# Sample rows through a DRAM scratch, a reordered key and value lane, denser squares in the first norm, and spreads by transposes, in a hybrid decoder step

## The chip, the core and the metric

The kernel runs on one core of a Trainium2 chip. The metric is the device time of one execution in microseconds (us). The engines run side by side and wait for one another only through semaphores: PE (TensorE, matmuls and transposes), DVE (VectorE), ACT (ScalarE), POOL (GpSimd), and SP (SyncE), which here issues every DMA.

## The reference

One layer of a decoder is computed for 256 prompt tokens and for 8 sample tokens (one new token for each of 8 sequences), together 264 columns. Cut to what matters here:

```python
# mixing sub-layer: x <- x + concat(out_A, out_B) @ w_out
proj = rmsnorm(x) @ w_in                         # [u | v_A | q | k | v | g]
out_A = gelu(u) * chunk_spatial_mix(layernorm(gelu(v_A)))
# retention, 8 heads of 128; for a sample token b and head h:
state[b] = gamma_h * state[b] + outer(k[b], v[b])     # 128 x 128
ret[b] = q[b] @ state[b]
out_B = silu(g) * groupnorm(ret)
# cross-attention, 4 heads of 512, 256 memory tokens; each sample token has its own cache
q = rmsnorm(x) @ w_cq
s[b] = cache_k[b] @ q[b] * 512 ** -0.5           # 256 scores
o[b] = softmax(s[b]) @ cache_v[b]
x = x + o @ w_co
# MLP and the last norm
x = x + relu(rmsnorm(x) @ w_ff1) ** 2 @ w_ff2
y = rmsnorm(x)
```

For the prompt, memory keys and values are computed from `mem_prompt` with `w_ck` and `w_cv`; they are outputs too, as are the retention states.

## The kernel before

**Weights.** Activations lie transposed: features on the 128 partitions, the 264 tokens along the free axis (sample tokens first, columns 0 to 7). All weight matrices are cut into chunks of 256 x 512 (512 KB); there are 512 of them in a fixed order: `w_in` (12 groups of 8 chunks, in the order v, q, k, q, k, v, vA, vA, g, g, u, u), `w_out`, `w_cq`, `w_ck` and `w_cv` in turn for four heads, `w_co`, then the MLP. `emit_dma` loads a chunk six ahead into one of five raw buffers, `emit_hi` casts it to fp32r on ACT, and `emit_lo` subtracts that on DVE to get the remainder; both are written two to three chunks ahead, into four buffers each. Every product is then three fp32r matmuls: high times high, high times low, low times high (L152 to L154 in `group_act`, L176 to L178 in `group_mem`). A group ends with four accumulators in PSUM, out of five banks; `evict` empties them on DVE and ACT, and the next group needs those banks.

**Order.** Between matmuls stand *points*, one after each six weight matmuls of `group_act`. At each point `run_point` (L210) advances every due generator of `chains`, then at most one of `tasks`, then issues due stores. A generator's `yield n` lets n points pass, a bare `yield` three. Tasks with a `lane` run in turn. All engines have their instructions in this written order, SP its DMAs too: an instruction that waits holds up what stands behind it on its engine.

**First norm.** The chunks of x are squared without the norm's factor, which is multiplied in behind the projection. `square_x` (L325) squares four tiles of 128 x 1056 on ACT and adds them on DVE; `column` sums over partitions with matmuls against ones and takes the power -1/2 on POOL; `tables` (L370) spreads the factor over the partitions (`spread`, L275: one matmul for each of three token blocks, the column broadcast as weights against the identity) and multiplies the rotary tables by it. Query and key evictions (`ev_rope`, L523) need those tables.

**Retention** (`retention`, L569) is one generator for each head, two lanes (`r0`, `r1`). For the sample tokens it transposes 8 columns of k and q into rows, casts them to a high part (rows 0 to 7 of `kq`) and a low part (rows 32 to 39), and then for each token a matmul with the selection column `sel[:, b]` broadcast (L619) puts row b, high plus low, on all 128 partitions of a PSUM tile `bc`. Two DVE instructions for each token then update the state (L622) and multiply it by q with a sum (L625).

**Sample attention** (`sample_attn`, L807) is one generator for each head in the lane `kv`. It makes split rows `qs` of the head's query in the same way; for each token a matmul (L820) spreads the row into `qb`, and two DVE products with the cached key tile (L823) give the scores. After a softmax the probabilities become split rows `pst`, spread by L843 into `pb`, and four DVE products with the cached value tile (L846) give the output. Key and value tiles (512 KB each) are loaded three ahead by `kv_fill` (L749), eight keys then eight values of each head in turn. Each key token takes five points, each value token four.

**Prompt attention** (`prompt_attn`) runs as a task put in front, once a head's memory keys and values are there. Before the seventh chunk of `w_co` all tasks are run out by `flush`.

Of the kernel before, what the change touches and what calls it, by code (L numbers as in the profile page):

```python
# [30 lines left out]
def build(tc, I, O):  # L31
# [5 lines left out]
    with cst as cst, wpool as wpool, spool as spool, tpool as tpool, psum as psum:  # L37
        with tc.manual_schedule():
            _emit(tc, cst, wpool, spool, tpool, psum, I, O)


def _emit(tc, cst, wpool, spool, tpool, psum, I, O):
# [41 lines left out]
    sel = cst.tile([128, 8], F32R, name="sel")  # L84
# [115 lines left out]
    def store(dst, src, delay=10):  # L200
        stores.append((now[0] + delay, dst, src))
# [8 lines left out]
    def run_point():  # L210
# [23 lines left out]
    class Stats:  # L234
# [40 lines left out]
        def spread(self, out, tok=TOK):  # L275
            ps = misc([128, self.n], "rsb")
            for i, (c0, n) in enumerate(tok):
                pe.matmul(ps[:, c0:c0 + n], lhsT=self.col[:, i:i + 1].broadcast_to([128, 128]),
                          rhs=ident[:, 0:n], start=True, stop=True)
            if out is None:  # L280
                return ps
            act.copy(out, ps[:])
# [42 lines left out]
    def square_x():  # L325
        a = slot([128, 4, T], "sqa")
        act.activation(a[:], hT[0][:], AF.Square)
        yield
        for s in range(1, 4):
            b = slot([128, 4, T], "sqb")  # L330
            act.activation(b[:], hT[s][:], AF.Square)
            yield 2
            dve.tensor_tensor(out=a[:], in0=a[:], in1=b[:], op=ALU.add)
            yield
        dve.tensor_tensor(out=a[:, 0:2, :], in0=a[:, 0:2, :], in1=a[:, 2:4, :], op=ALU.add)
        dve.tensor_tensor(out=st1.acc[:], in0=a[:, 0, :], in1=a[:, 1, :], op=ALU.add)
        yield 3
        st1.column()
        yield 4
        tables()  # L340
        for m in R4:
# [8 lines left out]
    def clear():  # L350
        zt = half("zt")
        dve.memset(zt[:], 0.0)
        S["kq"] = [S["rpool"].tile([128, 256], F32R, name="kq", tag="kq", bufs=2) for _ in range(2)]
        yield
        for i in range(2):
            act.copy(S["kq"][i][:], zt[:, 0:256])
        dve.tensor_tensor(out=sel[:], in0=ident[:, 0:8], in1=ident[:, 32:40], op=ALU.add)
# [127 lines left out]
    mix = {}  # L485
# [27 lines left out]
    def ev_rope(which, g):  # L513
        def ev(ps):
# [10 lines left out]
            def gen():  # L525
# [7 lines left out]
                if which == "k" and g == 0:  # L533
                    retentions(0)
# [33 lines left out]

    def retention(h):  # L569
# [6 lines left out]

        kn, vn = row("kn"), row("vn")
        sm = S["rpool"].tile([128, 384], F32, name="sm", tag="sm", bufs=2)
        kq = S["kq"][h % 2]
        tp = misc([128, 512], "tp")  # L580
# [3 lines left out]
        for i, src in enumerate((kt, qt)):  # L584
# [627 lines left out]
```

## Time and profile before

| what | value |
|---|---|
| time, median of 3 runs | 1603.66 us (1603.24 to 1604.05) |
| the profiled execution: time | 1604.01 us |
| its span, first to last instruction | 1602.1 us |
| mean granted clock of TensorE | 0.997 |
| busy: PE, DVE, ACT, POOL | 1587.7, 1040.8, 751.2, 124.1 us |
| moved by DMA | 326.15 MB, mean 204 GB/s |

How to read the views: the page's head gives the busy time of each engine with its share of the span and its instructions. The timeline lists instructions in the order of time: start, length, engine, line and operation, output and inputs, shape, count; in brackets the idle time of the engine before it and what ended it. The windows view gives, for stretches of time, each engine's busy time with its number of instructions, then the granted clock of TensorE, the mean busy share of the 16 DMA engines, and the rate. The list of groups has busy time and the mean length of one in ns, then the idle time just before such instructions and what ended it. The list of waits tells who waited for whom: total us, times, longest. The list of DMA issues gives count, size and the median us from issue to landing.

### The profile page before, as it was taken

To read this page: it belongs to the slowest core of one execution; us is meant where nothing else is said; L and a number is where in the kernel's file an instruction comes from. 1 tells how busy PE (TensorE), PEld (TensorE's weight loads), DVE (VectorE), ACT (ScalarE), POOL (GpSimd) and SP (SyncE) were. 2 spreads that over 40 slices of the span, in tenths; PEclk is the share of its full clock that TensorE was granted. 3 is DMA by queue.
4 is the path that set the end of the run, shared out by engine and by line. 5 is a ranking of instruction groups with operands and counts; after the bars stand their busy time and mean duration, and the time that the engine had idled before them with its cause. 6 is when DMAs were issued, how large, how long until landed. Compare 5 with 4: busy or idle time off the path is not lost.

```text
span 1602.1 us, 31005 instructions
## 1 busy us (share of the span) xinstructions
PE 1587.7 (99%) x12608; PEld 1560.0 (97%) x12608; DVE 1040.8 (65%) x1885; ACT 751.2 (47%) x1169; POOL 124.1 (8%) x111
## 2 busy tenths in 40 slices
PE   9999999999999999999999999999999999999997
PEld 8999999999999998999999999999999999999997
DVE  6677688678658777877655555555655555565555
ACT  6455566457444444444444543534444353444443
POOL 0242022010012201010000000000000000000000
PEclk9999999999999999999999999999999999999999
DMA  8566646465578887877555556565555655555552
GB/s 293 168 204 228 207 168 198 145 189 207 196 256 284 314 303 277 283 282 250 171 185 185 179 172 190 171 187 183 177 186 172 190 172 186 183 178 183 173 186 86
DMA packets 94222, 326.15 MB, mean 204 GB/s; under 512 B 10608, under 2 KB 15728, under 8 KB 94080
## 3 DMA queue, kind: packets, MB, share of 16 engines
q1 hardware_dynamic: 94080, 324.18, 60.8%
q8 instruction: 98, 1.61, 0.4%
q14 instruction: 44, 0.36, 0.1%
HBM read 313.03 MB, written 11.11 MB: 202 GB/s over the span
## 4 chain that ended last, share of the span: by engine, by line
PE 48%; issue 46%; DVE 1%; POOL 0%; ACT 0%; POOLq 0%; DVEq 0%
PE acc L152 13%; PE acc L153 13%; PE acc L154 13%; PE acc L178 2%; PE acc L177 2%; PE acc L176 2%; PE tp L96 1%; PE qb L820 0%; PE bc L619 0%; PE spp L474 0%; PE sc L898 0%; PE sc L896 0%; PE op L919 0%; PE sc L897 0%; PE op L921 0%
## 5 line engine op out<-in xcount | busy, mean ns | idle before, releaser
L1033 ACT CAST wh<-w 128x1024 fp32r<-128x1024 f32 (+1 forms) x513 | 536.1, 1045 | 712.1 <-PE acc L153 625.8
L1041 DVE TENSOR_TENSOR wl<-w,wh 128x1024 fp32r<-128x1024 f32 (+1 forms) x513 | 628.1, 1236 | 259.5 <-ACT wh L1033 257.5
L153 PE MATMUL acc<-h2l,wh 128*128 128x264 f32 x1024 | 291.2, 284 | 0.0
L152 PE MATMUL acc<-h2h,wh 128*128 128x264 f32 x1024 | 291.1, 284 | 0.0
L154 PE MATMUL acc<-h2h,wl 128*128 128x264 f32 x1024 | 290.6, 284 | 0.0
L153 PE MATMUL acc<-rl,wh 128*128 128x264 f32 x992 | 282.2, 284 | 0.0
L154 PE MATMUL acc<-rh,wl 128*128 128x264 f32 x992 | 282.1, 284 | 0.0
L152 PE MATMUL acc<-rh,wh 128*128 128x264 f32 x992 | 282.0, 284 | 0.0
L152 PE MATMUL acc<-xh,wh 128*128 128x264 f32 x768 | 225.1, 293 | 3.2 <-DVE ra L523 2.5
L154 PE MATMUL acc<-xh,wl 128*128 128x264 f32 x768 | 219.3, 286 | 0.4 <-DVE wl L1061 0.2
L153 PE MATMUL acc<-xl,wh 128*128 128x264 f32 x768 | 219.0, 285 | 0.1
L152 PEld LDWEIGHTS acc<-h2h,wh 128*128 128x128 f32 x1024 | 192.7, 188 | 0.0
L153 PEld LDWEIGHTS acc<-h2l,wh 128*128 128x128 f32 x1024 | 192.7, 188 | 0.0
L154 PEld LDWEIGHTS acc<-h2h,wl 128*128 128x128 f32 x1024 | 192.6, 188 | 0.0
L152 PEld LDWEIGHTS acc<-rh,wh 128*128 128x128 f32 x992 | 186.9, 188 | 0.0
L153 PEld LDWEIGHTS acc<-rl,wh 128*128 128x128 f32 x992 | 186.7, 188 | 0.0
L154 PEld LDWEIGHTS acc<-rh,wl 128*128 128x128 f32 x992 | 186.5, 188 | 0.0
L152 PEld LDWEIGHTS acc<-xh,wh 128*128 128x128 f32 x768 | 145.3, 189 | 5.8 <-DVE ra L523 3.2
L154 PEld LDWEIGHTS acc<-xh,wl 128*128 128x128 f32 x768 | 145.3, 189 | 0.9 <-DVE wl L1061 0.4
L153 PEld LDWEIGHTS acc<-xl,wh 128*128 128x128 f32 x768 | 145.5, 189 | 0.3 <-DVE xl L104 0.3
L951 DVE TENSOR_TENSOR hT<-hT,acc 128x264 f32<-128x264 f32 x124 | 53.2, 429 | 73.7 <-PE acc L154 73.7
L92 POOL TENSOR_TENSOR msr<-msv,neghalf 128x3 f32<-128x3 f32 (+1 forms) x5 | 7.7, 1547 | 991.5 <-DVE msv L265 739.1
(253 smaller groups left out, 2776.5 us busy)
## 6 DMA issues: line engine op xcount, KB each, us to landing
w<-in_w_ff_dram SPq DMA_DIRECT2D x256, 512.0 KB, 4.1
w<-in_w_in_dram SPq DMA_DIRECT2D x95, 512.0 KB, 3.8
w<-in_w_out_dram SPq DMA_DIRECT2D x32, 512.0 KB, 4.2
w<-in_w_cq_dram SPq DMA_DIRECT2D x32, 512.0 KB, 4.5
kv<-in_kN_dram SPq DMA_DIRECT2D x32, 512.0 KB, 5.2
kv<-in_vT_dram SPq DMA_DIRECT2D x32, 512.0 KB, 4.9
w<-in_w_ck_dram SPq DMA_DIRECT2D x32, 512.0 KB, 5.5
w<-in_w_cv_dram SPq DMA_DIRECT2D x32, 512.0 KB, 4.7
```

The costliest lines, as they stand in the source:

```text
L92: gp.tensor_tensor(out=out, in0=in_, in1=neghalf[0:in_.shape[0], 0:n], op=ALU.pow)
L96: pe.transpose(out, in_, ident[0:p, 0:p])
L152: pe.matmul(ps, lhsT=a, rhs=xh, start=(i == 0), stop=False)
L153: pe.matmul(ps, lhsT=a, rhs=xl, start=False, stop=False)
L154: pe.matmul(ps, lhsT=b, rhs=xh, start=False, stop=(i == nk - 1))
L176: pe.matmul(ps, lhsT=a, rhs=hi[:, k, :], start=(kt == 0), stop=False)
L177: pe.matmul(ps, lhsT=a, rhs=lo[:, k, :], start=False, stop=False)
L178: pe.matmul(ps, lhsT=b, rhs=hi[:, k, :], start=False, stop=(kt == 15))
L951: dve.tensor_tensor(out=h[m], in0=h[m], in1=ps[m][:], op=ALU.add)
L1033: act.copy(hi[:, k, :], raws[i][:, k, :])
L1041: dve.tensor_tensor(out=lo[:, k, :], in0=raw[:, k, :], in1=hi[:, k, :].bitcast(F32), op=ALU.subtract)
```

## The change

Five things change.

1. *Retention's sample rows.* `sample_rows(g)`, a task after each key group, gathers the 8 sample columns of four heads of k and of q, transposes them (two transposes give 32 rows of k and of q), and stores the 32 x 256 rows into a DRAM scratch. `rows_of` loads two tokens' rows from there onto all 128 partitions (256 KB), one step ahead, into one of four buffers. The matmuls L619, the split rows `kq` and `sel` go. A step of two tokens takes three points instead of two; some other waits in the generator become shorter, and it now waits until the store has been issued.
2. *Sample attention's rows.* `sample_q` takes one transpose of a head's 128 x 32 query columns and stores the rows to DRAM; after the softmax the probabilities are stored too. `kv_fill` also keeps a second queue `rowq` of up to three rows, each loaded onto all 128 partitions (2 KB of a query, 1 KB of probabilities). The matmuls L820 and L843 and the split rows go.
3. *Order of the lane.* `sample_attn` becomes `sample_k` and `sample_v`; the tiles come as K0 K1 V0 K2 V1 K3 V2 V3, so that the softmax of a head passes while the next head's keys are multiplied.
4. *First norm.* The squares and adds follow one another at one point each; the waits behind are shorter, and the values' multiplication comes two points after the tables.
5. *Spreads.* `spread` transposes the broadcast column, 128 columns for each token block, the last block first, instead of multiplying it by the identity.

The queue of stores no longer holds back a due store behind one that is not due.

```diff
     def store(dst, src, delay=10):
-        stores.append((now[0] + delay, dst, src))
+        e = [now[0] + delay, dst, src, False]
+        stores.append(e)
+        return e
...
-        while stores and stores[0][0] <= now[0]:
-            _, dst, src = stores.popleft()
-            sp.dma_start(out=dst, in_=src)
+        for e in [e for e in stores if e[0] <= now[0]]:
+            sp.dma_start(out=e[1], in_=e[2])
+            e[3] = True
+            stores.remove(e)
...
         def spread(self, out, tok=TOK):
             ps = misc([128, self.n], "rsb")
-            for i, (c0, n) in enumerate(tok):
-                pe.matmul(ps[:, c0:c0 + n], lhsT=self.col[:, i:i + 1].broadcast_to([128, 128]),
-                          rhs=ident[:, 0:n], start=True, stop=True)
+            for i, (c0, _) in reversed(list(enumerate(tok))):
+                transpose(ps[:, c0:c0 + 128], self.col[:, i:i + 1].broadcast_to([128, 128]))
...
     def square_x():
-        a = slot([128, 4, T], "sqa")
-        act.activation(a[:], hT[0][:], AF.Square)
-        yield
-        for s in range(1, 4):
-            b = slot([128, 4, T], "sqb")
+        q = []
+        for s in R4:
+            b = slot([128, 4, T], "sqa")
             act.activation(b[:], hT[s][:], AF.Square)
-            yield 2
-            dve.tensor_tensor(out=a[:], in0=a[:], in1=b[:], op=ALU.add)
-            yield
+            q.append(b)
+            yield 1
+            if s:
+                dve.tensor_tensor(out=q[0][:], in0=q[0][:], in1=q.pop()[:], op=ALU.add)
+                yield 1
+        a = q[0]
...
-        yield 3
+        yield 2
         st1.column()
         yield 4
         tables()
+        yield 2
...
+    def sample_rows(g):
...
+        cols = S["rpool"].tile([128, 2, 32], F32, name="kqcol", tag="kqcol", bufs=1)
+        for i, w in enumerate("kq"):
+            act.copy(cols[:, i, :].rearrange("p (m b) -> p m b", m=4), S[w][g][:, :, 0:8])
+        yield 2
+        tp = misc([32, 2, 128], "tp")
+        for i in range(2):
+            transpose(tp[:, i, :], cols[:, i, :])
+        rows = S["rpool"].tile([32, 256], F32, name="kqrow", tag="kqrow", bufs=1)
+        act.copy(rows[:], tp[:].rearrange("p a d -> p (a d)"))
+        S["kqd"][g] = dpool.tile([32, 256], F32, name=f"kqd{g}")
+        S["kqe"][g] = store(S["kqd"][g][:], rows[:], 3)
+        yield
+
+    def rows_of(h, b0):
+        t = S["rpool"].tile([128, 2, 256], F32, name="bkq", tag="bkq", bufs=4)
+        r = 8 * (h % 4) + b0
+        sp.dma_start(out=t[:].rearrange("p b f -> p (b f)"),
+                     in_=S["kqd"][h // 4][r:r + 2, :].rearrange("b f -> (b f)").partition_broadcast(128))
+        return t
...
     def retention(h):
...
+        while g not in S["kqe"] or not S["kqe"][g][3]:
+            yield 2
+        yield 2
+        ahead = rows_of(h, 0)
...
-        for i, src in enumerate((kt, qt)):
-            transpose(tp[0:8, 256 + i * 128:384 + i * 128], src[:, 0:8])
...
-        act.copy(kq[0:8, :], tp[0:8, 256:512])
-        dve.tensor_tensor(out=kq[32:40, :], in0=tp[0:8, 256:512], in1=kq[0:8, :].bitcast(F32), op=ALU.subtract)
...
-            bc = misc([128, 2, 256], "bc")
-            for j in range(2):
-                b = b0 + j
-                pe.matmul(bc[:, j, :], lhsT=sel[:, b:b + 1].broadcast_to([128, 128]), rhs=kq[:], start=True, stop=True)
+            bc = ahead
+            if b0 < 6:
+                ahead = rows_of(h, b0 + 2)
...
-            yield 2
+            yield 3
...
-        yield 16
+        yield 12
...
-    kv_list = [(w, h, b) for h in R4 for w in ("kN", "vT") for b in range(8)]
+    kv_list = [(w, h, b) for w, h in (("kN", 0), ("kN", 1), ("vT", 0), ("kN", 2), ("vT", 1), ("kN", 3), ("vT", 2), ("vT", 3))
+               for b in range(8)]
...
+        while row_next[0] < len(kv_list) and len(rowq) < KV_AHEAD:
+            w, h, b = kv_list[row_next[0]]
+            if (w, h) not in rowsrc or not rowsrc[w, h][0][3]:
+                break
+            t = S["mpool"].tile([128, 512], F32, name="brow", tag="brow", bufs=KV_AHEAD)
+            n = 512 if w == "kN" else 256
+            sp.dma_start(out=t[:, 0:n], in_=rowsrc[w, h][1][b].partition_broadcast(128))
+            rowq.append(t)
+            row_next[0] += 1
...
-            defer(sample_attn(h), 4, lane="kv")
+            defer(sample_q(h), 4, front=True)
+            defer(sample_k(h), 12, lane="kv")
+            if h > 0:
+                defer(sample_v(h - 1), 1, lane="kv")
+            if h == 3:
+                defer(sample_v(3), 1, lane="kv")
...
+    def sample_q(h):
+        tp = misc([32, 128], "tp")
+        transpose(tp[:], q8[h][:].rearrange("p m b -> p (m b)"))
+        q32 = half("q32")[0:32, 0:128]
+        act.copy(q32, tp[:])
+        qd = dpool.tile([8, 512], F32, name=f"qd{h}")
+        e = store(qd[:].rearrange("b (m d) -> m b d", m=4), q32, 2)
+        rowsrc["kN", h] = (e, qd)
+        yield 3
+        kv_fill()
...
+            kc, qb = kvq.popleft(), rowq.popleft()
...
+            def keep(p):
+                pd = dpool.tile([8, 256], F32, name=f"pd{h}")
+                rowsrc["vT", h] = (store(pd[:], p[0:8, :], 2), pd)
+                yield 3
+                kv_fill()
```

More of the change, by code (lines that the diff above doesn't have):

```diff
@@ L532, in gen @@
                     dve.tensor_tensor(out=o[:, m, :], in0=o[:, m, :], in1=a[m][:], op=ALU.add)
-                if which == "k" and g == 0:
-                    retentions(0)
+                if which == "k":
+                    defer(sample_rows(g), 2)
+                    if g == 0:
+                        retentions(0)
             chain(gen())
@@ L663, in retention @@
         act.activation(vt, tp[:], AF.Copy, scale=halfgn[:, h:h + 1])
+        done.add(h)
     def ev_g(g):
@@ L805, in softmax, with rows_ready, sample_k @@
         return ex
-    def sample_attn(h):
-        qs, pst = S["qs"], S["pst"]
-        tp = misc([8, 512], "tp")
-        for m in R4:
-            transpose(tp[:, m * 128:(m + 1) * 128], q8[h][:, m, :])
-        act.copy(qs[0:8, :], tp[:])
-        dve.tensor_tensor(out=qs[32:40, :], in0=tp[:], in1=qs[0:8, :].bitcast(F32), op=ALU.subtract)
+    def sample_q(h):
[8 more added lines that the diff above has]
+        kv_fill()
+    def rows_ready():
+        kv_fill()
+        n = 0
+        while not rowq:
+            n = 1
+            yield 3
+            kv_fill()
+        if n:
+            yield 8
+    def sample_k(h):
         sc = small(16, "scs")
-        yield
+        yield from rows_ready()
         for b in range(8):
             kv_fill()
-            kc = kvq.popleft()
-            qb = misc([128, 512], "qb")
-            pe.matmul(qb[:], lhsT=sel[:, b:b + 1].broadcast_to([128, 128]), rhs=qs[:], start=True, stop=True)
+            kc, qb = kvq.popleft(), rowq.popleft()
             for i in range(2):
@@ L826, in sample_attn, with scores, sample_v @@
             kv_fill()
-        tp = misc([8, 256], "tp")
-        for i in range(2):
-            transpose(tp[:, i * 128:(i + 1) * 128], sc[:, i * 8:(i + 1) * 8])
-        def spread_p(p):
-            act.copy(pst[0:8, :], p[0:8, :])
-            yield 2
-            dve.tensor_tensor(out=pst[32:40, :], in0=p[0:8, :], in1=pst[0:8, :].bitcast(F32), op=ALU.subtract)
-        softmax(tp[:], 8, spread_p)
-        yield 11
+        def scores():
+            tp = misc([8, 256], "tp")
+            for i in range(2):
+                transpose(tp[:, i * 128:(i + 1) * 128], sc[:, i * 8:(i + 1) * 8])
+            def keep(p):
+                pd = dpool.tile([8, 256], F32, name=f"pd{h}")
+                rowsrc["vT", h] = (store(pd[:], p[0:8, :], 2), pd)
+                yield 3
+                kv_fill()
+            softmax(tp[:], 8, keep)
+            yield
+        defer(scores(), 3, front=True)
+    def sample_v(h):
+        yield from rows_ready()
         so = S["mpool"].tile([128, 4, 8], F32, name="so", tag="so", bufs=4)
@@ L840, in sample_attn @@
             kv_fill()
[L841 to L843 removed]
+            vc, pb = kvq.popleft(), rowq.popleft()
             for d in R4:
                 jk = half("vjk")
[L846 to L847 removed]
+                dve.scalar_tensor_tensor(out=jk[:, 0:256], in0=vc[:, d * 256:(d + 1) * 256], scalar=1.0,
+                                         in1=pb[:, 0:256], op0=ALU.mult, op1=ALU.mult, accum_out=so[:, d, b:b + 1])
             yield 4
```

41 lines of the change are left out of this document (13 added, 28 removed).

## The prediction

> **What bounds the kernel now.** I read the page's head first, then the chain that ended last, then TensorE alone in the order of time, then the DMA by stage.
>
> ```profile
> span 1602.1 us, 31005 instructions
> PE 1587.7 (99%) x12608; PEld 1560.0 (97%) x12608; DVE 1040.8 (65%) x1885; ACT 751.2 (47%) x1169; POOL 124.1 (8%) x111
> PE 48%; issue 46%; DVE 1%; POOL 0%; ACT 0%; POOLq 0%; DVEq 0%
> 1000.00:1100.00 100.00, 100.00 (x823) 100.00 (x823) 55.46 (x71) 42.33 (x53) 0.00 (x0) 1.00 0.57 176
> ```
>
> The last line is a stretch of the windows view (length, then PE, PEld, DVE, ACT, POOL busy with counts, granted clock, DMA share, GB/s). TensorE holds the span: the chain is PE and its own issue for 94%, and in the feed-forward stage 823 matmuls of 264 columns fill 100 us, one every 0.1215 us. The stated length of one (0.28 us) is latency; what an instruction costs is how far it moves the next start. So an instruction taken from TensorE is worth its start-to-start time, provided that nothing else becomes late. The profiled execution took 1604.01 us, 1.9 us more than its span and 0.35 us over the median of 1603.66; I sum against 1604.0.
>
> **What leaves TensorE.** First the broadcasts of sample rows, from the timeline (start, length, instruction) and the tile view (shortest, median and longest ns, first and last start):
>
> ```profile
> 103.48 0.39 PE L619 MATMUL bc<-kq,sel 128*128 128x256 f32 x2
> 103.70 0.29 PE L152 MATMUL acc<-xh,wh 128*128 128x264 f32 x1
> ...
> 463.10 0.39 PE L820 MATMUL qb<-qs,sel 128*128 128x512 f32 x1
> 463.33 0.28 PE L152 MATMUL acc<-h1h,wh 128*128 128x264 f32 x1
> ...
> 502.39 0.28 PE L843 MATMUL pb<-pst,sel 128*128 128x256 f32 x1
> 502.51 0.29 PE L152 MATMUL acc<-h1h,wh 128*128 128x264 f32 x1
> L619 PE MATMUL bc<-kq,sel x64: 275/278/283, 103.5 to 246.1; 128*128 128x256 f32 x64
> L820 PE MATMUL qb<-qs,sel x32: 389/392/401, 463.1 to 708.9; 128*128 128x512 f32 x32
> L843 PE MATMUL pb<-pst,sel x32: 277/279/287, 502.4 to 743.2; 128*128 128x256 f32 x32
> ```
>
> Retention: 32 pairs at 0.22 = 7.0 us. Keys: 32 x 0.23 = 7.4 us. Values: 32 x 0.12 = 3.8 us. All lie on TensorE between weight matmuls, so all of it comes off: 18.2 us.
>
> Then the transposes and the spreads:
>
> ```profile
> 92.91 0.49 PE L96 MATMUL tp<-cmat,k 128*128 128x128 f32 x3
> 93.46 0.28 PE L153 MATMUL acc<-xl,wh 128*128 128x264 f32 x1
> ...
> 95.54 0.38 PE L96 MATMUL tp<-cmat,vt 128*128 128x128 f32 x2
> 95.88 0.29 PE L153 MATMUL acc<-xl,wh 128*128 128x264 f32 x1
> ...
> 460.46 0.60 PE L96 MATMUL tp<-cmat,q 128*8 128x128 f32 x4
> 461.02 0.29 PE L153 MATMUL acc<-h1l,wh 128*128 128x264 f32 x1
> ...
> 51.40 0.73 PE L278 MATMUL rsb<-cmat,msr 128*128 128x128 f32 x6
> 52.19 0.28 PE L153 MATMUL acc<-xl,wh 128*128 128x264 f32 x1
> ```
>
> Read against the second weight matmul behind (the first is shifted too), less the 0.12 us that one weight matmul takes: three k transposes and one q cost 0.55 - 0.12 = 0.43 us, two vt transposes 0.34 - 0.12 = 0.22, four q transposes 0.44, so 0.11 us each whatever the columns kept. A spread is six records (each plain matmul runs as two) for 0.79 - 0.12 = 0.67 us.
> - Retention loses 16 eight-column transposes (1.7 us), `sample_rows` adds 2 x 2 (0.4 us): 1.3 us.
> - The query goes from 16 transposes to 4: 1.3 us by the rate, 1.0 us taken, since a lone one may pay the change of type alone.
> - A spread becomes three transposes, 0.33 us. Three in mid-kernel save 0.34 each, the memory's (four records to two) 0.2: 1.2 us. At the end two spreads stand in front of the last multiplication; three records fewer before its start are about 0.35 us.
>
> The other engines lose the casts and subtractions that built the split rows and gain a few copies. I cost that at nothing: DVE and ACT are busy 65% and 47%. DVE's products of rows keep shapes and count but read SBUF instead of PSUM; from rows of like shape (`hT` adding from PSUM, `rl` within SBUF) I take them as equal:
>
> ```profile
> L951 DVE TENSOR_TENSOR hT<-hT,acc 128x264 f32<-128x264 f32 x124 | 53.2, 429 | 73.7 <-PE acc L154 73.7
> L943 DVE TENSOR_TENSOR rl<-r,rh 128x264 fp32r<-128x264 f32 x64 | 24.8, 430 | 5.2 <-ACT r L940 5.2
> ```
>
> **The first norm.** Squares and sums are spread over 18 points of the order now and over 7 afterwards; with the shorter waits behind them the tables come 12 points sooner. A point is six weight matmuls, 0.73 us, so 8.8 us. What that is worth:
>
> ```profile
> 58.40 0.39 PE L152 MATMUL acc<-xh,wh 128*128 128x264 f32 x1 [1.79 <-DVE ra L523]
> 56.00:58.00 2.00, 0.62 (x6) 0.40 (x4) 2.00 (x3) 1.25 (x2) 1.87 (x3) 1.00 0.00 0
> 58.00:64.00 6.00, 5.60 (x33) 5.60 (x34) 5.62 (x9) 1.04 (x1) 5.73 (x5) 0.72 0.62 190
> ```
>
> The third group finds its banks taken: DVE (2.00 of 2.00 busy) is still at tables, `vt` and weight splits when it should empty them. TensorE stands some 1.9 us, and then the granted clock falls to 0.72 over the next 6 us, 1.7 us lost. With tables 8.8 us earlier both go: 3.6 us. What is late next is a weight split behind the denser adds, which has two chunks (5.8 us) in hand. I add 0.5 us for retention's kq subtraction, which no longer stands before evictions.
>
> Off TensorE: 18.2 + 1.3 + 1.0 + 1.2 + 0.35 + 3.6 + 0.5, about 26 us.
>
> **What the change adds: waits on SP and DVE.** SP issues 32 row loads in retention and 64 in attention, and ten small stores. Such a store stands on SP until ACT has made its rows, and the first load behind it until the store has landed; weight loads queue behind both.
>
> ```profile
> SPq L1027 <- DVE wl L1041: 1095.4, 446, 7.7
> w<-in_w_in_dram SPq DMA_DIRECT2D x2, 256.0 KB, 3.6
> dec<-in_c_dec_dram SPq DMA_DIRECT2D x8, 128.0 KB, 5.0
> DVE state L622 <- PE bc L619: 8.4, 9, 2.6
> ```
>
> SP has time: it mostly waits for a weight split to free a raw buffer (1095 us), and what it then loads is needed only four chunks (11.6 us) later. So only the first wait of a stage (K0 and retention's two) can bite; later rows are stored long before their turn. I take no cost, and 1 us for K0 at most.
>
> In retention DVE waits for a row load issued one step (three points, 2.2 us) earlier, plus SP's lead of up to a chunk (2.9). The nearest landings are 3.6 and 5.0 us: a wait of 0 to 2.8 us. DVE's 8.4 us of waiting for broadcasts go. TensorE feels a wait only where it stands before the evictions at one of seven group ends in retention; 32 steps x 2.8 us in 171 us cover half the time, so 10 us is the far end, and -1 the near one. I take +2, nearer the low end because of SP's lead.
>
> **The attention stage's DMA** is the largest unknown. The lane of sample attention lasts from 463 to 745 us. Afterwards it needs no pause for the softmax: 4 x (40 + 32) points of 0.73 us, with a start, contending tasks and three heads' prompt attention (48 matmuls each, 17 us), about 230 us.
>
> ```profile
> 460.00:745.00 285.00, 285.00 (x1999) 265.95 (x1998) 224.65 (x572) 127.28 (x193) 43.05 (x35) 1.00 0.83 290
> 730.00:740.00 10.00, 10.00 (x48) 8.26 (x47) 9.08 (x36) 4.05 (x5) 0.00 (x0) 1.00 1.00 394
> 196.00:200.00 4.00, 4.00 (x36) 4.00 (x35) 2.93 (x6) 4.00 (x10) 0.00 (x0) 1.00 0.99 292
> kv<-in_kN_dram SPq DMA_DIRECT2D x32, 512.0 KB, 5.2
> out_mem_k_dram<-kz SPq DMA_DIRECT2D x16, 128.0 KB, 5.9
> ```
>
> In these 230 us go 64 key and value tiles of 512 KB (33.6 MB), about 73 weight chunks as large (38.3), three heads' memory keys and values out (3.1), and new: 32 rows of 2 KB and 32 of 1 KB, each to 128 partitions (12.6 MB). 87.6 MB in 230 us are 381 GB/s; the stage moves 290 now. The best stretch of 10 us here moved 394 at a full share: no loss. But a row spread over partitions may be dearer than its bytes. The one such load that the trace has (`bbc`, 0.52 MB) falls into 196 to 200 us, where full engines moved 292 GB/s, 0.41 MB less than at 394. Laid wholly on it, spread rows cost 1.8 times their bytes: 10.1 MB more, 248 us, a loss of 18. Half of that gives 235 us. I take 6 us, nearer to the low end, since 394 is this stage's own rate and stores share those 4 us; buffers (five weights, three tiles) cover short excesses. DVE, 224.65 us busy in 285, would be some 87% busy in the shorter stage.
>
> Sum: 1604.0 - 26 + 2 + 6 = 1586.
>
> **Rivals.**
> - A, nothing becomes late: 1604 - 26 - 1 = 1577. For it: 394 GB/s above, and rows asked for three ahead. Against it: 381 is the mean of phases, and a value step (four points, 2.9 us) asks 1.18 MB, 407 GB/s.
> - B, retention's DVE waits at the group ends: the 10 us above, 1594. For it: four buffers for two lanes, and landings up to 5.0. Against it: SP's lead.
> - C, attention is bound by DMA, at what the mean share suggests. 0.83 busy at 290 GB/s is 349 at full share: 251 us, a loss of 21, 1601, no change that shows: 0.2% of 1603.66 is 3.2 us, about what a measurement can tell. Against it: 394 GB/s over 10 us. Beside it stands a rule of the Trainium skill (DMA: Bandwidth & Descriptors, Specifications): memory gives one core about 358 GB/s, below the fabric. By that the stage takes 245 us and the kernel about 1595. The trace's 394 lies above it, for 10 us only.
> - D, slower: as C, and half the surcharge on spread rows: 92.6 MB at 349 GB/s are 265 us, 35 lost, 1615. It decides from a loss of 27 us on, that is if the stage sustains less than 360 GB/s with that surcharge. DVE then waits for tiles and rows, the splits and evictions behind them come late, and TensorE stands. For it: the 292 GB/s above, and K1 ahead of V0, which leaves no pause in which DMA catches up.
> - E, the first norm's stall stays, because the denser adds push DVE's splits into the eviction: 1589.6.
>
> **How the numbers follow.** Forecast with its own range of 1580 to 1592: 0.50. A 0.18, B 0.12, E 0.04, all faster; C 0.06, the same; D 0.10, slower. Faster 0.84, same 0.06, slower 0.10. The range from 1576.5 to 1600 leaves out C, D and a little below A. The time is the forecast's.
>
> **What would show it.** TensorE's instruction count falls by 128 + 12 + 12 + 17 or so. No idle TensorE near 56 us and no clock below 1.00 at 60 us: the first norm. DVE's `state` waiting for DMA instead of `bc`: retention; the same before evictions makes B. `kjk` and `vjk` waiting for DMA, a DMA share at 1.00 through 470 to 700 us and fewer matmuls than 7.1 per us there: C or D. The last `vjk` near 700 us tells whether the lane really runs without pauses. Wrong I would be above all by the rate of spread rows.

## The result and the profile after

The changed kernel takes 1617.95 us (median; 1613.11 to 1620.56) against 1603.45 us (1603.03 to 1604.05) for the kernel before on the same chip: a ratio of 1.0087 [1.0075, 1.0099], slower by 14.5 us. Forecast were 1586 us. The profiled execution took 1618.36 us, with a span of 1616.6 and a mean granted clock of 0.990, where before had 0.997. The head of its page, and the chain that ended last:

```profile
span 1616.6 us, 30757 instructions
PE 1578.3 (98%) x12439; PEld 1549.9 (96%) x12439; DVE 1044.4 (65%) x1866; ACT 745.1 (46%) x1159; POOL 130.0 (8%) x111
issue 46%; PE 10%; DVE 5%; DMA 4%; SPq 0%; POOL 0%; DVEq 0%; ACT 0%; POOLq 0%
```

TensorE lost the 169 instructions that were to go (12608 to 12439). But the chain, which was PE and its issue for 94% of the span, now goes through DVE and DMA for 9% (the shares listed add up to 65%). A tally of the span: TensorE is busy 1578.3 us of 1616.6, so it stands 38.3 us; before it stood 1602.1 - 1587.7 = 14.4. That is 23.9 us more. The granted clock costs 1616.6 x 0.010 = 16.2 us against 1602.1 x 0.003 = 4.8, 11.4 more (within about 1 us, since the clock is given to three places). The span grew by 14.5, so the work itself shrank by 23.9 + 11.4 - 14.5 = 20.8 us. The saving is there; new idle time and a slower clock took it all and 14.5 us more.

Whom TensorE waited for, and below it three of DVE's waits (total us, times, longest us):

```profile
PE tp L96 <- DVE kn L676: 13.0, 5, 3.3
PE tp L96 <- DVE ex L832: 3.9, 2, 3.0
PE msq L273 <- DVE sq L339: 2.5, 1, 2.5
PE acc L154 <- DVE wl L1091: 2.3, 3, 1.8
...
DVE kjk L868 <- DMA brow<-qd: 19.7, 15, 2.9
DVE vjk L896 <- DMA brow<-pd: 7.8, 7, 2.9
DVE state L643 <- DMA bkq<-kqd: 7.7, 5, 2.6
```

None of TensorE's four stood in the list of before with more than 0.2 us. They belong to retention's norm, to a softmax and a weight split in the attention stage, and to the first norm. The stretches in which they fall, and two whole stages (length, then PE, PEld, DVE, ACT, POOL busy with counts, granted clock, DMA share, GB/s):

```profile
40.00:42.00 2.00, 0.25 (x2) 0.25 (x3) 1.67 (x3) 0.00 (x0) 0.00 (x0) 1.00 0.22 43
42.00:46.00 4.00, 4.00 (x22) 4.00 (x22) 1.31 (x2) 1.05 (x1) 1.78 (x1) 0.57 0.43 159
120.00:126.00 6.00, 5.00 (x42) 4.81 (x41) 5.39 (x20) 0.39 (x3) 0.00 (x0) 1.00 0.98 356
134.00:138.00 4.00, 4.00 (x23) 3.92 (x21) 1.82 (x5) 1.77 (x8) 0.00 (x0) 0.57 0.97 226
150.00:156.00 6.00, 5.70 (x32) 5.53 (x33) 5.14 (x15) 2.64 (x4) 0.00 (x0) 0.72 0.36 119
179.00:186.00 7.00, 6.37 (x30) 6.04 (x31) 3.45 (x9) 2.28 (x8) 0.00 (x0) 0.53 0.58 187
222.00:227.00 5.00, 4.78 (x24) 4.43 (x25) 3.13 (x8) 1.45 (x8) 0.00 (x0) 0.66 0.55 197
262.00:268.00 6.00, 4.05 (x32) 3.64 (x32) 4.39 (x14) 2.55 (x8) 0.00 (x0) 1.00 0.59 210
519.00:525.00 6.00, 4.42 (x37) 4.22 (x36) 5.04 (x7) 4.23 (x12) 4.40 (x4) 1.00 1.03 409
602.00:606.00 4.00, 4.00 (x22) 4.00 (x23) 3.44 (x13) 1.68 (x4) 0.00 (x0) 0.57 1.00 364
700.00:706.00 6.00, 5.41 (x33) 5.41 (x33) 5.35 (x15) 3.39 (x5) 1.82 (x1) 0.72 1.03 406
95.00:290.00 195.00, 180.80 (x1399) 176.66 (x1398) 139.42 (x383) 105.04 (x247) 36.27 (x38) 0.96 0.69 228
470.00:700.00 230.00, 222.14 (x1557) 207.25 (x1555) 191.29 (x462) 98.54 (x156) 44.59 (x30) 0.99 0.95 346
```

Read the second row: TensorE is busy all 4 us and starts only 22 matmuls, at a mean clock of 0.57. So it ran at half clock for 3.4 us and lost 1.7. Seven rows are like that; length x (1 - clock) over them gives 1.7 + 1.7 + 1.7 + 3.3 + 1.7 + 1.7 + 1.7 = 13.5 us. Before had one such place in its middle, at 58 to 64 us. Each of the seven begins within some 2 us of a place where TensorE had stood for 2.1 to 3.5 us from one start to the next.

The three stalls in the timeline (start, length, engine, line; in brackets the idle time before and what ended it):

```profile
40.53 0.70 DVE L338 TENSOR_TENSOR sqa<-sqa 128x528 f32<-128x528 f32 x1
41.27 0.43 DVE L339 TENSOR_TENSOR sq<-sqa 128x264 f32<-128x264 f32 x1
41.75 1.24 PE L273 MATMUL msq<-ones,sq 128*128 128x128 f32 x6 [2.53 <-DVE sq L339]
...
141.56 7.29 POOL L526 TENSOR_TENSOR k<-z,tab 64x264 f32<-64x264 f32 x8 [9.15 <-ACT z L520]
144.12 0.71 DVE L671 TENSOR_SCALAR gva<-gs 128x3 f32<-128x3 f32 x1
148.93 0.85 POOL L92 TENSOR_TENSOR grs<-gva,neghalf 128x3 f32<-128x3 f32 x1
149.81 0.84 DVE L676 TENSOR_SCALAR kn<-kn,gnm,grs 128x128 f32<-128x128 f32 x3 [4.98 <-POOL grs L92]
150.30 0.65 PE L96 MATMUL tp<-cmat,kn 128*128 128x128 f32 x3 [3.04 <-DVE kn L676]
...
592.14 0.69 DVE L868 SCALAR_TENSOR_TENSOR kjk<-kv,brow 128x512 f32<-128x512 f32 x1 [2.00 <-DMA brow<-qd]
601.48 0.35 DVE L832 TENSOR_SCALAR ex<-ex,rc 128x256 f32<-128x256 f32 x1
601.89 0.81 PE L96 MATMUL tp<-cmat,ex 128*128 128x128 f32 x3 [3.01 <-DVE ex L832]
```

- *First norm.* The sum over partitions (L273) stands in TensorE's order two points, 1.5 us, behind the last add. DVE makes the adds back to back, gets to the last at 41.27, and TensorE stands 2.53 us.
- *Retention.* The norm's variance `gva` is ready at 144.8. The power on POOL stands behind eight rotary products (7.29 us) until 148.93, DVE normalises at 149.81, and the transposes of `kn`, which now stand 12 points behind the norm's start and not 16, hold TensorE 3.04 us. It is a place where TensorE waits for five engine steps, and the new distance is four points, 2.9 us, shorter; the five waits are 2.6 us each in the mean. Before, this head (the second) had its `kn` 2.9 us ahead of the transposes:

```profile
141.67 1.47 DVE L656 TENSOR_SCALAR kn<-kn,gnm,grs 128x128 f32<-128x128 f32 x3
146.02 0.53 PE L96 MATMUL tp<-cmat,kn 128*128 128x128 f32 x3
```

- *Attention.* DVE waits 2.00 us for a row of the query, then works off what has piled up; a weight split among that takes 3.41 us instead of 1.22, beside POOL's `vl` (593.14 to 595.71 us). The prompt's softmax behind it is normalised at 601.48, and its transposes hold TensorE 3.01 us.

Where the time went by stage. A stage runs from the start of its first product to that of the next one's, as in these two rows (the attention stage is 754.5 - 445.2 = 309.3 us), beside the last value product, which the prediction had put near 700 us:

```profile
L152 PE MATMUL acc<-h1h,wh x256: 280/283/371, 445.2 to 541.7; 128*128 128x264 f32 x128
L152 PE MATMUL acc<-oh,wh x256: 279/284/367, 754.5 to 854.0; 128*128 128x264 f32 x128
L896 DVE SCALAR_TENSOR_TENSOR vjk<-kv,brow x128: 405/418/2612, 540.7 to 727.6; 128x256 f32<-128x256 f32 x128
```

| stage, us | before | after | `b0_mends` | `b1_pace` |
|---|---|---|---|---|
| start to the fourth group of w_in (first norm) | 82.7 | 83.1 | 79.3 | 79.7 |
| to w_out (retention) | 255.8 | 267.8 | 248.6 | 248.0 |
| w_out | 94.4 | 94.3 | 94.3 | 94.3 |
| w_cq to w_co (attention) | 306.7 | 309.3 | 307.4 | 295.1 |
| w_co | 99.7 | 99.9 | 99.9 | 101.4 |
| MLP and last norm | 762.8 | 762.2 | 762.4 | 762.4 |

The last two columns are kernels of the next section. Retention has lost 12.0 us and attention 2.6; each of the three stages that the change touches should have become shorter.

### The profile page after: what moved, and what is told of

The parts are those of the page before. It is cut to its first block, busy times and chain, and to the rows that moved or that the text cites. A ratio compares the mean times of both kernels' runs of the same rounds, so it can differ in the third digit from the quotient of the medians.

```text
span 1616.6 us, 30757 instructions
## 1 busy us (share of the span) xinstructions
PE 1578.3 (98%) x12439; PEld 1549.9 (96%) x12439; DVE 1044.4 (65%) x1866; ACT 745.1 (46%) x1159; POOL 130.0 (8%) x111
## 4 chain that ended last, share of the span: by engine, by line
issue 46%; PE 10%; DVE 5%; DMA 4%; SPq 0%; POOL 0%; DVEq 0%; ACT 0%; POOLq 0%
PE acc L152 3%; PE acc L153 3%; PE acc L154 3%; DMA brow<-qd 2%; DVE wl L1091 2%; DVE vjk L896 1%; DMA brow<-pd 1%; DMA w<-in_w_cv_dram 1%; DVE kjk L868 1%; PE acc L177 0%; PE acc L178 0%; PE acc L176 0%; DMA kv<-in_kN_dram 0%; DMA w<-in_w_ck_dram 0%; DVE kz L907 0%
## 5 line engine op out<-in xcount | busy, mean ns | idle before, releaser
L92 POOL TENSOR_TENSOR msr<-msv,neghalf 128x3 f32<-128x3 f32 (+1 forms) x5 | 7.7, 1548 | 985.7 <-DVE msv L268 738.9
```

What stands on the lines that cost most here:

```text
L92: gp.tensor_tensor(out=out, in0=in_, in1=neghalf[0:in_.shape[0], 0:n], op=ALU.pow)
```

## The experiments

The runs were taken on several chips, on which the kernel before took 1602.9 to 1604.2 us in the median; differences between kernels of different chips are good to about 1 us.

**Retention's wait alone** (`e1_wait16`). The changed kernel with the old distance in front of the norm's transposes:

```diff
-        yield 12
+        yield 16
         tp = misc([128, T], "tp")
```

> The changed kernel with retention's wait ahead of the last transposes put back from 12 to 16 points; all else stays. In the profile of the changed kernel TensorE waits five times, 13.0 us in all, in those transposes for the group norm on DVE, and the granted clock is halved for 17 us in that stage (8.5 us lost). Theory 1 (the shortened wait): the five waits and the halved clock go, about 21 us: 1597, retention back to 100 us for some 820 to 825 matmuls. Theory 2 (the group norm is late because DVE waits for row loads, 7.7 us in the list of waits): the waits on the group norm become shorter by the 2.9 us they get at best where they are, but the DVE's lateness comes out elsewhere, before evictions; gain under 8 us, 1610 or more.

Measured: 1599.14 us (1595.12 to 1600.69), ratio to before 0.9968 [0.9955, 0.9981]; 18.8 us below the changed kernel. The waits for `kn` are gone, and the window of retention has its matmuls and its clock back:

```profile
95.00:290.00 195.00, 192.46 (x1554) 188.44 (x1553) 156.32 (x413) 112.29 (x260) 38.99 (x38) 1.00 0.70 243
```

13.0 us of waits and four places of half clock (1.7 + 1.7 + 3.3 + 1.7 = 8.4) stood there, 21 together; by the profiles the stage falls from 267.8 to 247.8 us. One number in one line turned the change from a gain to a loss. The other theory, that the row loads hold retention, falls: they are unchanged here. But the old distance is only just enough now. Before, all eight heads had their `kn` ready 2.9 to 5.1 us ahead of the transposes; here it is 0.0 to 6.2 us, and the second head has nothing left. Counted from that head's transpose of `rs_t`, the power on POOL was done after 7.6 us before, ahead of the eight rotary products of k; here it comes behind them and is done after 13.9.

**The first norm's sum, later** (`e2_column7`). The sum and the power go seven points behind the last add; retention stays at 12:

```diff
-        yield 2
+        yield 7
         st1.column()
```

> The changed kernel with the first norm's sum over partitions 7 points behind the last add instead of 2 (the tables stay 7 points earlier than before the change). Theory 1 (the matmul of the sum is placed ahead of DVE's adds and holds up TensorE): the 2.5 us of waiting at 39 us and the half clock behind it (1.7 us) go, and no wait comes at the query eviction: about 4 us less than the changed kernel, 1614. Theory 2 (DVE is short of time in this stage, so the stall only moves to the query's eviction as before the change): a wait on the evictions near 56 us comes back, no gain.

Measured: 1612.15 us (1605.73 to 1614.19), ratio 1.0049 [1.0033, 1.0064]; 5.8 below the changed kernel. At the same place TensorE runs at full clock, 35 matmuls where it had 22:

```profile
42.00:46.00 4.00, 4.00 (x35) 4.00 (x35) 2.58 (x4) 1.05 (x1) 1.73 (x1) 1.00 0.71 259
```

The stage is 79.2 us against 83.1. The stall and its half clock are 2.5 + 1.7 = 4.2 us. The rest of the 5.8 is no gain of this edit that could be told from the spreads of some 8 us that both kernels have: the same edit on top of `e1_wait16` (`b0_mends` below) is worth 4.3.

**The attention stage put back** (`e3_attn_old`). The changed kernel, but with sample attention as before: order of tiles, split rows, matmuls L820 and L843. The diff is the second and third part of the change, reversed:

```diff
-    kv_list = [(w, h, b) for w, h in (("kN", 0), ("kN", 1), ("vT", 0), ("kN", 2), ...
+    kv_list = [(w, h, b) for h in R4 for w in ("kN", "vT") for b in range(8)]
...
-            defer(sample_q(h), 4, front=True)
-            defer(sample_k(h), 12, lane="kv")
...
+            defer(sample_attn(h), 4, lane="kv")
```

> The changed kernel with sample attention put back whole: split rows spread by matmuls, keys and values of a head in turn, no row queue. In the profile of the changed kernel TensorE waits 9.4 us in attention and loses 3.4 us to half clock. Theory 1 (attention loses to DMA about what it takes off TensorE, 12.2 us): within 3 us of the changed kernel, 1615 to 1621, and DMA falls from 350 to 376 GB/s in those slices back to about 300. Theory 2 (attention is what makes the change slow): at least 8 us faster, below 1610. Theory 3 (attention gains nearly all that was forecast): at least 8 us slower, 1626 or more.

Measured: 1612.67 us (1611.53 to 1613.7), ratio 1.0058 [1.0041, 1.0075]; 5.3 below the changed kernel. The two profiled runs lie 6.8 us apart; of these the attention stage gives 2.7 (306.5 against 309.3) and retention, which the edit leaves alone, 4.1 (263.7 against 267.8). So the net loss in attention is about 3 us rather than 5, as `b5_attn_old` below confirms, where a gain of 6.2 was forecast. The time lies between two of the expectations, and DMA is back at 294 GB/s: attention bears part of the loss, retention most of it.

**Who makes retention's norm late** (`e4_recip`, one run). The distance stays 12; the power on POOL is replaced by a reciprocal on DVE, which is other arithmetic of the same size:

```diff
-            rsqrt(rs[:], va[:], 3)
+            dve.reciprocal(rs[:], va[:])
```

> The changed kernel with the power -1/2 of retention's group norm on POOL replaced by a reciprocal on DVE (it leaves out the square root); the wait stays at 12 points. Theory 1a (the group norm is late because its power stands on POOL behind the rotary products, 7.3 us for eight): the longest waits, 3 us and more, go; the waits of TensorE for the group norm fall from 13.0 us to below 6. Theory 1b (the chain ACT to DVE is too long for 12 points even without POOL): they stay above 9 us.

Measured: 1614.41 us in one run, 1612.6 of span against 1616.6. TensorE's waits for `kn`:

```profile
PE tp L96 <- DVE kn L676: 8.9, 4, 4.0
```

13.0 us have become 8.9, and the longest wait has not become shorter. The second head's wait of 3.04 us is gone, so there it was POOL's queue of rotary products. The first and fifth heads still wait 2.36 and 3.95 us (2.00 and 3.26 in the changed kernel). With one run, and 11.6 to 13.0 us of such waits in the three kernels that keep 12 points and the power on POOL, POOL's share is a third at most; what else makes those heads late was not taken apart. Neither expectation alone holds.

**Both mends** (`b0_mends`): `yield 16` and `yield 7` together, the base of all kernels below.

> The changed kernel with both mends: retention's last wait at 16 points, and the first norm's sum 7 points behind the last add. The parts touch different stages, so the gains add up: by the stages of the profiles (from the start to the fourth group, from there to w_out) 79.1 and 247.8 us, against 82.6 and 255.7 before the change; attention is as in the changed kernel, 309 to 311 us against 306.7. Theory 1 (what is left of the change is a gain of some 11 us in mixing, and attention gives back 2 to 4): 1593 to 1596. Theory 2 (a mend opens another stall, since the lateness is DVE's): 1598 or more.

Measured: 1594.89 us (1593.68 to 1595.12), ratio 0.9945 [0.9929, 0.9962]. First norm and retention now take 79.3 and 248.6 us, 3.4 and 7.2 less than before. Most of what is left of the 8.9 us to 1586 lies in attention: 307.4 us, where 306.7 - 12.2 + 6 = 300.5 were forecast. Whom DVE waited for there, and the window of the stage:

```profile
DVE kjk L868 <- DMA brow<-qd: 17.3, 11, 3.0
DVE vjk L896 <- DMA brow<-pd: 7.8, 8, 2.5
```

```profile
470.00:700.00 230.00, 220.99 (x1548) 205.80 (x1547) 198.18 (x509) 100.24 (x159) 46.16 (x27) 0.99 0.97 357
```

DMA is at 0.97 of its share, DVE waits 25 us for rows, and there are 1548 matmuls in 230 us, 6.7 per us, where before had 1632.

**A slower lane** (`b1_pace`). Each key token takes six points, not five, each value token five, not four:

```diff
 # sample_k
-            yield 5
+            yield 6
 # sample_v
-            yield 4
+            yield 5
```

> As b0_mends, with sample attention's lane slower: six points for each key token and five for each value token instead of five and four. The same bytes, matmuls and products, over about a fifth more time. Theory 1 (attention asks more of DMA in the shorter lane than it gives): the share of DMA falls below 0.95 there, the waits of TensorE for ex, wl and kz (9 to 10 us) go, and the stage from w_cq to w_co falls from 309 to 311 us to 297 to 301: 8 to 12 us less than b0_mends. Theory 2 (row loads are late by their own landing, whatever the rate): less than 3 us.

Measured: 1582.12 us (1581.83 to 1582.75), ratio 0.9866 [0.9851, 0.9881]. It beats both kernels, by some 21 and 36 us, and `b0_mends` by 12.8, a little more than the first theory had. TensorE's waits for `ex`, `wl` and `kz`, 8.9 us in `b0_mends`, are at 0.2; the share of DMA did not fall below 0.95. The same views, and the last value product:

```profile
DVE kjk L868 <- DMA brow<-qd: 8.9, 6, 3.5
DVE vjk L896 <- DMA brow<-pd: 5.2, 4, 2.5
```

```profile
470.00:700.00 230.00, 229.11 (x1630) 215.33 (x1629) 193.58 (x443) 106.36 (x166) 41.25 (x31) 1.00 0.95 341
```

```profile
L896 DVE SCALAR_TENSOR_TENSOR vjk<-kv,brow x128: 404/418/1001, 528.0 to 741.7; 128x256 f32<-128x256 f32 x128
```

The lane ends 39 us later than in `b0_mends` (702.7) and the kernel 12.8 us earlier. What the lane asks for accounts for much of it. A weight chunk is 0.524 MB in 24 matmuls, 2.92 us, 180 GB/s. A key step adds a tile and a row of 2 KB to 128 partitions, 0.786 MB in 3.65 us, 216 GB/s; a value step 0.655 MB in 2.92 us, 225. Together 396 and 405 GB/s. At six and five points they ask 180 + 179 = 359 in both. At its share of 0.95 to 0.97 the stage moves 341 to 357 GB/s, so 359 to 368 at a full share: the first pace is beyond it, the second just at it. Transfers are then late in bursts, and a late row holds DVE and through it TensorE.

A second thing changes with the pace, and no run separates the two. The row products now have both inputs in SBUF, and beside a long instruction of POOL (`vl`, four times in the kernel) such a product can stand until POOL is done; before, with the row in PSUM, it did not. Two rows of before, then two of the changed kernel:

```profile
742.45 2.39 POOL L884 TENSOR_TENSOR vl<-vnat,vh 128x1024 fp32r<-128x1024 f32 x1 [20.29 <-ACT vh L882]
743.51 0.42 DVE L846 SCALAR_TENSOR_TENSOR vjk<-kv,pb 128x256 f32<-128x256 f32 x1 [0.23 <-PE pb L843]
...
649.55 2.86 POOL L934 TENSOR_TENSOR vl<-vnat,vh 128x1024 fp32r<-128x1024 f32 x1 [21.32 <-ACT vh L932]
650.08 2.88 DVE L868 SCALAR_TENSOR_TENSOR kjk<-kv,brow 128x512 f32<-128x512 f32 x1
```

A `kjk` takes 0.69 us else. In `b0_mends` three row products are caught so, each some 2.2 us longer; in `b1_pace` one, by 0.6 (the 1001 ns in its row of `vjk`).

**Rows from many places** (`b2_plain`). As `b0_mends`, but each row load takes 128 different rows of an input with as many bytes; so what is multiplied is not the row wanted.

```diff
-            sp.dma_start(out=t[:, 0:n], in_=rowsrc[w, h][1][b].partition_broadcast(128))
+            sp.dma_start(out=t[:, 0:n], in_=I[w][h, b][:, 0:n])
```

> As b0_mends, but in attention the row tiles are loaded from 128 different rows of the key and value caches instead of one row spread over 128 partitions: the same sizes and count, other data (it leaves out the spreading of the query and of the probabilities; nothing waits for the DRAM rows). Theory 1 (a spread row is dearer than its bytes, up to 1.8 times, by the forecast): DMA moves the same bytes in less time, the waits of DVE for brow (27 us) fall by half or more and the stage is 4 us shorter or more. Theory 2 (only the bytes count): the stage stays within 2 us of b0_mends.

Measured: 1588.38 us (two runs near 1585.8, two near 1591.5), ratio 0.9906 [0.9886, 0.9927], 6.5 below `b0_mends`; the profiled run is one of the slower two (1590.89), and its stage takes 305.3 us against 307.4.

```profile
470.00:700.00 230.00, 223.18 (x1565) 209.18 (x1564) 199.54 (x519) 100.88 (x160) 44.85 (x27) 0.99 0.94 354
```

So the stage stays full with plain rows as well (0.94). The packets themselves tell the surcharge: those of 2 KB, which bring the query rows, took 104 ns in the mean in `b0_mends` and 88 here, with a median of 84 in both, so a row read 128 times cost about 1.2 times its bytes. The time may hold something else too, since these loads don't wait for a store to DRAM either. A surcharge of 0.8 times the bytes, the far end of the prediction, would have been worth 10.1 MB, 28 us at 354 GB/s.

**No rows at all** (`b4_norows`). One buffer of rows is loaded once and used by every step, so scores and outputs are made of the wrong rows; all else moves as in `b0_mends`:

```diff
-            t = S["mpool"].tile([128, 512], F32, name="brow", tag="brow", bufs=KV_AHEAD)
+            t = S["brow"]
```

> As b0_mends, but attention's row loads are left out: all products read one row tile, loaded once (it leaves out the spreading of query and probabilities). TensorE, DVE, the order and the other loads stay. Theory 1 (the row loads, 12.6 MB more in this stage, are what makes DMA late): the stage falls from 309 to 311 us to 294 to 297, what the matmuls taken away are worth (12 us), and the time to 1579 to 1583. Theory 2 (the lane without pauses is too dense for DVE or for the key and value tiles alone): it falls by less than 6 us.

Measured: 1583.18 us (1582.43 to 1583.67), ratio 0.9872 [0.9857, 0.9886]; the stage takes 297.9 us, 9.5 less than in `b0_mends`.

```profile
470.00:700.00 230.00, 227.02 (x1617) 213.32 (x1616) 204.36 (x528) 104.70 (x166) 52.95 (x29) 1.00 0.84 310
```

The 12.6 MB of rows cost 11.7 us at the fast pace, and the share falls to 0.84 without them. `b1_pace`, with all of its rows, takes no longer than this, and its stage is even 2.8 us shorter: the fast lane loses 3 us or so without any rows. Two row products caught beside `vl` are in this trace as well (2.24 and 2.61 us); some 8 us behind the second, TensorE stands 1.72 us.

**The old order of tiles** (`b3_order`). As `b0_mends`, rows through DRAM, but eight keys and eight values of each head in turn:

```diff
-    kv_list = [(w, h, b) for w, h in (("kN", 0), ("kN", 1), ("vT", 0), ("kN", 2), ...
+    kv_list = [(w, h, b) for w, h in [(w, h) for h in R4 for w in ("kN", "vT")]
                for b in range(8)]
...
             defer(sample_k(h), 12, lane="kv")
-            if h > 0:
-                defer(sample_v(h - 1), 1, lane="kv")
-            if h == 3:
-                defer(sample_v(3), 1, lane="kv")
+            defer(sample_v(h), 1, lane="kv")
```

> As b0_mends, but with the lane's tiles in the old order, K0 V0 K1 V1 K2 V2 K3 V3: rows still come through DRAM, and each head's values again wait for its own softmax and the landing of its probabilities, so that DMA gets pauses. Theory 1 (it is the density of the lane, not the row loads as such, that makes DMA late): the stage from w_cq to w_co falls from 307.4 us to 296 to 300, nearly as with the slower pace (295.1). Theory 2 (the order does not matter): within 2 us of 307.4. Theory 3 (the pauses make the lane too long, and the rest is run out without matmuls ahead of w_co's seventh chunk): the stage falls, but the stage of w_co (99.9 us) grows by more than 3.

Measured: 1590.08 us (1588.61 to 1591.18), ratio 0.9921 [0.9906, 0.9936].

```profile
470.00:700.00 230.00, 225.88 (x1598) 212.11 (x1597) 189.80 (x448) 101.14 (x157) 35.02 (x27) 0.99 0.90 332
```

The pauses for the softmax do what rival D says of them: DMA catches up (0.90), and the stage takes 301.1 us, 6.3 less, a little short of the first theory's 296 to 300. But the lane becomes too long, its last value product is at 747.6 us, and the w_co stage takes 104.1 us, 4.2 more: it stands for the attention's outputs `oh`.

```profile
PE acc L152 <- ACT oh L100: 2.8, 1, 2.8
```

At the fast pace the old order is thus better by some 4 to 5 us (the two were taken on different chips). What the new order brings is an earlier end of the lane, and `b1_pace` spends that on a slower pace. The old order at the slower pace wasn't tried; with as many tokens and more points for each, its lane should end later still.

**Attention as before, with the mends** (`b5_attn_old`): `b0_mends` with the edit of `e3_attn_old`.

> As b0_mends, with sample attention as before the change (rows spread by matmuls, old order, old pace). It is the reference for what rows through DRAM are worth in attention once the other two stalls are mended. From the stages: 79.2 + 248.6 + 94.3 + 306.5 + 99.8 us against 839.1 before, so 10.7 us less than before: 1592 to 1594. Theory 1 (the rows are worth 10 us or more if the lane leaves DMA room): b1_pace (1582.1) stays 9 to 12 us below it, and b0_mends, with the dense lane, 0 to 3 us above it. Theory 2 (the pace alone, not the rows, made the gain of b1_pace): this kernel lies within 3 us of b1_pace.

Measured: 1591.93 us (1591.2 to 1592.08), ratio 0.9932 [0.9915, 0.9949]. The new attention at its own pace loses 3.0 us against this, at the slower pace it gains 9.8: as the first theory had it.

## Why the prediction was wrong, point by point

**The step that failed** is a term put at nothing without a reason: the distances in retention's generator. The description of the change says that "some other waits in the generator become shorter", and the diff shows `yield 16` becoming `yield 12`. The part on retention costs matmuls, transposes, a subtraction and row loads, and no distance. It cost 18.8 us (`e1_wait16`), more than half of the 32 us between forecast and result. By stage, forecast and result are 79.1 and 83.1 us (first norm), 249.0 and 267.8 (retention), 300.5 and 309.3 (attention).

Would the rows of before have told it? No wait for `kn` stood in TensorE's list, and the timeline of before shows the cover: 2.9 to 5.1 us from the last `kn` to its transposes, over the eight heads. A cut of four points, 2.9 us, just uses that up where it is smallest. So the cut alone, with all else in its old place, would have cost little by these rows (no run has it alone). What turned it into stalls, by the traces, is that the rest of the change moved the heads against the key and query groups: with the old distance back, two heads have 1.0 us or less in hand. The distance and what comes to stand inside it had to be looked at together.

**What leaves TensorE** was right. 18.2 + 1.3 + 1.0 + 1.2 + 0.35 = 22.1 us of work were forecast; the tally of after gives 20.8, good to a microsecond or so. In `b1_pace` the same tally gives 20.9: the span is 21.1 us shorter than before's, TensorE stands 17.4 us (3.0 more) and the clock costs 1.6 (3.2 less).

**The first norm.** The old stall near 56 us went, and the gain of 3.6 us came true once the new one was mended: the stage is 3.4 us shorter in `b0_mends`. "What is late next is a weight split behind the denser adds, which has two chunks (5.8 us) in hand" named the wrong thing: late next was the sum itself, which TensorE takes 1.5 us behind the last add. Rival E foresaw a stall in the first norm, by the splits and not by the sum, and with 1589.6 as its end.

**Retention's rows.** The 2 us came out in size: with the mend the stage is 7.2 us shorter, and -7.0 - 1.3 - 0.5 + 2 is -6.8. They were not felt only where the prediction put them. DVE did come to wait for row loads, 7.7 us in the changed kernel, but TensorE stood for it in retention's own transposes of rows (`PE rp L96 <- DVE bkq L645`, 1.0 us there and 1.8 in `b0_mends`, 0.2 for the like wait before) and at the evictions 0.2 us (`ra`; 1.4 in `b0_mends` with `vt`). Rival B had a place and a price for a wait of retention's, at the wrong instruction.

**The attention stage's DMA** was mis-sized. The saving there is 7.4 + 3.8 + 1.0 = 12.2 us, so a stage without loss would take 294.5. It takes 309.3, a loss of 14.8 where 6 was taken; 12.9 with the mends (307.4); 0.6 with the slower pace, and 1.7 in the w_co stage behind it. The step that failed is "nearer to the low end, since 394 is this stage's own rate". A stretch of 10 us is not a rate that 230 us keep up: the stage moved 346 GB/s at a share of 0.95 there, which is 364 when full. Rival C's 349 was the better figure; the Trainium skill's rule beside it (DMA: Bandwidth & Descriptors, Specifications, about 358 GB/s of memory for one core) lies close to the 341 to 357 that the full stage kept over 230 us, though single stretches of 6 us moved more, such as the 409 above. Not all of the loss need be DMA's rate.

**Taken as equal.** The prediction took DVE's products of rows as equal whether the row is read from PSUM or SBUF. The medians are (417 and 418 ns for `vjk`), but the longest `vjk` went from 424 to 2612 ns, beside POOL's `vl`. What that cost of the stage's loss is open.

**Spread rows.** The loss was feared from 1.8 times the bytes. The packets show about 1.2 times. Taking the spreading away is worth 6.5 us of time (from runs that spread over 6) and 2.1 of the stage, taking the rows away 11.7 and 9.5: by the stage, most of it is bytes.

**The rivals.** The time lies 3 us from D's 1615, but by chance, and not by D's mechanism. D asked for 35 us of loss in attention; that stage bore 14.8, and retention, which D left alone, bore the most. What C and D said of DVE ("waits for tiles and rows, the splits and evictions behind them come late, and TensorE stands") is much what the timeline shows at 592 to 602 us, though there TensorE stands for the prompt's softmax. A came within reach only as `b1_pace`, 1582.

**What would show it.** Of the signs named, the count of instructions came out exactly, and no idle time near 56 us. `state` waited for DMA, a share near 1 and fewer than 7.1 matmuls per us came as C and D had them. The last value product at 727.6 us was late mainly because the stage began late, at 445.2 us; in `b0_mends` it begins at 422.2, and the last product is at 702.7.

## What to carry to other kernels

In a hand-ordered kernel a changed distance is a change like any other: for each one list who must have finished by the shorter time, down to an engine's in-order queue. Where the list of waits shows none, the timeline still shows the cover, from the end of the writer to the start of the reader: compare the cut with the smallest of these, and take off what the rest of the change will put in between. Before raising the pace of a lane of loads, add up what all lanes ask in GB/s per step and hold it against the rate that the stage keeps over its whole length; a lane that asks 10% more than that is better slowed down, if its end has room. When an operand moves from PSUM to SBUF, look at what runs beside it, not at its median alone. Price a stall with the clock that may follow.

## What the runs showed of the hardware

The granted clock falls after short stalls, by where they fall. In the changed kernel's profile, behind its first microseconds, eight gaps between starts of TensorE were 2.06 to 3.54 us long. Behind seven of them half clock followed for 3.4 us, once for 6.8 (windows at 42, 134, 150, 179, 222, 602 and 700 us above); behind one, 2.24 us at 262 us, it did not, nor behind gaps of 1.3 and 1.9 us at 120 and 519 us. Those three windows show TensorE idle for 1.95, 1.00 and 1.58 us at a clock of 1.00.

The trace's record of the clock tells why. The seven slow stretches begin at 42.24, 134.40, 151.47, 178.78, 223.15, 602.03 and 701.02 us: the later six lie 27, 32, 40, 53, 164 and 193 times 3.4133 us behind the first. So in this trace the clock changes on a fixed grid of 3.41 us. Counted on such a grid in each trace, from 12 to 1575 us, the twelve traces of this case have 28 stretches at full clock with TensorE idle for 1.77 us or more, and half clock follows 27 of them; of the 39 with 1.0 to 1.73 us idle, it follows one. The idle 1.95 us at 262 us are divided between two stretches, 0.78 and 1.17. The first norm's stall shows it best: 2.53 us whole in one stretch in the changed kernel, which cost 4.2 us with the clock, and 2.54 us divided 1.64 and 0.90 in `e1_wait16`, where the clock stays:

```profile
42.00:46.00 4.00, 4.00 (x34) 4.00 (x34) 1.31 (x2) 1.05 (x1) 1.78 (x1) 1.00 0.48 163
```

The Trainium skill (TensorE: Matmul & The Clock Gate, Part 1) has the clock halve after an idle window of about 3.4 us that runs freely; the 3.4 us and the free run agree with these traces, but a stretch that was idle for about half was enough here. This may be why the changed kernel's runs spread over 7.5 us and those of `b1_pace`, with hardly a gap, over 0.9; no run tested that.

A DVE instruction with both inputs in SBUF stood until POOL's `vl` was done (2.88 us instead of 0.69 beside 2.86 us of POOL, above), while a product with its row in PSUM ran beside it at its usual 0.42 us.
